# A fourth group of seven products in the second pair of column blocks of two down projections

## The chip, the cores and the metric

The kernel runs on one core of one Trainium2 chip. Times are device microseconds (us) of one execution; the time of a kernel is the median over runs. The engines are named as in the profile: PE (matrix engine), PEld (its weight loads), DVE (vector engine), ACT (scalar engine), POOL (GpSimd) and SP (issues most transfers). Each engine works through its own queue in order; semaphores connect them.

## The reference, cut to what matters

One layer on 256 rows of width 2048, all in float32: a half-weighted feed-forward network (FFN), a mixer, a second such network, and a gated embedding. The change touches the down projection `@ w_down` of both networks.

```python
def swiglu(h, w_gate, w_up, w_down):
    return (jax.nn.silu(h @ w_gate) * (h @ w_up)) @ w_down

x = x + 0.5 * swiglu(rms_norm(x, ffn1_norm[i]), ffn1_w_gate[i], ffn1_w_up[i], ffn1_w_down[i])
...
x = x + 0.5 * swiglu(rms_norm(x, ffn2_norm[i]), ffn2_w_gate[i], ffn2_w_up[i], ffn2_w_down[i])
```

The hidden width is 5632, the output width 2048. A down projection is thus 256 x 5632 times 5632 x 2048.

## The kernel before

**Three matmuls for one product.** Every float32 operand is split into a high part that PE takes (ACT copies it, line 182) and a low part, the rest (DVE subtracts, line 185). A product is then high x high, low x high and high x low: three matmuls, each 128 x 128 weights against 128 x 512 columns. The weights of the model are the moving operand; they are split on the fly, in tiles of 128 x 1024 (two k tiles of 512 columns), with names `whi`/`wlo` or, from a second ring, `shi`/`slo`. The rings hold four and three such pairs.

**Quarters and column blocks.** The 5632 hidden entries are 11 "quarters" of 512 (four k tiles of 128); the 2048 output columns are four blocks of 512, done in two pairs. One transfer of 1 MB brings one quarter of one block into a `raw` tile (lines 343 and 557). There are five `raw` buffers; during a down stage two of them hold the rows of x that the result is added to, so three are left for weights.

**Two ways to do a quarter.** As *columns* (`column`, line 660): for one block, each half of the quarter is split once and used by both row tiles, 12 matmuls a half, 24 a block, 48 for both blocks, with 4 splits. As a *group* (`chunk`, line 635): both blocks together, by a scheme of Strassen's kind, with 7 products instead of 8, each of 6 matmuls, 42 in all. For it DVE makes three sums of weight tiles (t1, t2, t4, line 550), POOL adds a fourth one by an accumulating transfer (line 643), and all seven right-hand sides are split. The left-hand sums of a quarter are made by `sum_forms` (line 487): four small DVE operations (line 496) and a split. The tiles for t1, t2, t4 and for these left-hand sums (`rows`) share two buffers. The products add into eight banks of PSUM, numbered 1 to 8; the columns of the first block use banks 2 and 4, those of the second 3 and 8, the same ones as the groups, so that both ways add up.

**The plan of a stage.** In `ffn`, `plans` lists the order for each of the two pairs of blocks: `("c", k)` does quarter k as columns, first block then second; `("s", k)` as a group; `("f", k)` makes the left-hand sums for k ahead of time. The last entry closes the stage: in the second pair it is `("a", (5, 6, 7, 8))`, the first block over quarters 5, 6, 7, 8 and then the second over 8, 7, 6, 5. After the last group `opened` (line 811) takes the banks 1, 5, 6 and 7 out: one ACT copy and eight DVE operations of 512 columns. `end` adds the remaining banks of a block to x and starts the next stage's preparation of it.

The hidden activations are split per quarter by `act` (line 803; a DVE row `hlo<-hT`), and `kept` holds the last two quarters. The sums of quarters 1 and 2 are kept from the first pair of blocks; that of quarter 0 is made again.

**What sets the order.** The code is traced in program order, with `step()` between pieces of work, at which work put off earlier (`put_off`) is traced. A scheduler then orders the instructions of each engine: by program order, except where an instruction would have to wait and a later one need not, and except for those pinned to program order. On SP the transfers of weights and those of the turned activations share one queue.

Of the kernel before, what the change touches and what calls it, by code (L numbers as in the profile page):

```python
# [33 lines left out]
def layer_kernel(ctx: ExitStack, tc: tile.TileContext, a: dict, shapes: dict, out: bass.AP):  # L34
# [47 lines left out]
    def small(n=8):  # L82
        return smp.tile([P, 8], F32, tag="sm", name=uid("sm"))[:, :n]
# [24 lines left out]
    def put_off(steps, fn, *args):  # L108


        def g():
            for _ in range(steps):
                yield
            fn(*args)

        return start(g())
# [370 lines left out]
    def sum_forms(pool, u, kind="n"):  # L487

        sums = pool.tile([P, 2, NB], F32, tag="sum", name=uid("rows"), bufs=2)
        s = sums.rearrange("p j n -> p (j n)").rearrange("p (z j x b) -> p z j x b", z=4, j=2, b=32)  # L490
        (a11, a21), (a12, a22) = ([u[:, k : k + 2, 4 * t : 4 * t + 4] for t in range(TT)] for k in (0, 2))
        for z, (x, y, op) in enumerate((
            (a21, a22, ALU.subtract), (s[:, 0], a11, ALU.subtract),
            (a11, a21, ALU.subtract), (a12, s[:, 1], ALU.add),
        )):
            nc.vector.tensor_tensor(out=s[:, z], in0=x, in1=y, op=op)
        both = halves(kind)
        split(*both, sums.rearrange("p j n -> p (j n)").rearrange("p (z t) -> p z t", z=4))
        return both
# [175 lines left out]
    def ffn(i, xn, nxt, bg=None):  # L675
# [7 lines left out]
        side = ExitStack()  # L683
# [18 lines left out]
        for f in range(NF):  # L702
# [9 lines left out]
            if f >= early or f in alone:  # L712
# [17 lines left out]
                s = Seven(xn, lambda kb: sums[kb], ((wg, f * NB), (wu, f * NB)), sevens, turns)  # L730
# [69 lines left out]
        def rows(k):  # L800
            return hT[k // 2][:, k % 2 * 4 : k % 2 * 4 + 4]
# [6 lines left out]
        def gather(x, ps, scale):  # L808
            nc.vector.scalar_tensor_tensor(out=x, in0=ps, scalar=scale, in1=x, op0=ALU.mult, op1=ALU.add)

        def opened(s, n):
# [5 lines left out]
            for t in range(TT):  # L817
# [9 lines left out]
                ("c", 10),  # L827
            ),
            (
                ("c", 10), ("c", 9), ("s", 2), ("c", 3), ("s", 1), ("f", 0), ("c", 4), ("s", 0), ("a", (5, 6, 7, 8)),  # L830
            ),
        )
        parts, forms = {}, {}
# [13 lines left out]
        for n in range(0, ND, 2):  # L847

            def end(side):
                m = n + side  # L850
                for t, z in enumerate(((2, 4), (3, 8))[side]):
                    gather(xt[t][m], s.bank(z), 0.5)
                put_off(0 if m == ND - 2 or m == ND - 1 and m < nxt.early else 2, nxt.block, m)

            s = Seven(kept, summed, ((wd, n * NB), (wd, (n + 1) * NB)), sevens, turns)
            plan = plans[n // 2]
            left = sum(kind == "s" for kind, _ in plan)
            for kind, kb in plan:
                final = (kind, kb) == plan[-1]
                if kind == "f":  # L860
                    forms[kb] = sum_forms(sevens, rows(kb))
                    continue
                if kind == "s":
                    left -= 1
                    s.chunk(kb, () if left else shared)
                    if not left:
                        put_off(0, opened, s, n)
                    continue
                for side in range(2):
                    s.column(side, (kb,) if kind == "c" else kb[:: 1 - 2 * side], final)  # L870
                    if final:
                        end(side)
        pools.close()
# [737 lines left out]

    n1, nm, n2, npl = Normed("ffn1_norm", load_turned), Normed("mix_norm"), Normed("ffn2_norm", kinds="hhnn", late=0), Normed("ple_norm", late=0)
    ffn(1, n1, nm, s5_prep)

    w_in = a["w_in"]
# [75 lines left out]
    mix.close()  # L1691

    ffn(2, n2, npl)


# [62 lines left out]
    with sums_phase("sums3") as sevens:  # L1758
        forms = {1: sum_forms(sevens, whole_rows(sevens, npl(1)), "h")}
        s = Seven(npl, forms.get, ((wg, 0), (wg, NB)), sevens, sevens)  # L1760
# [31 lines left out]
    s = small(1)  # L1792
# [157 lines left out]
```

## Time and profile before

| | us |
|---|---|
| median of three runs | 1808.87 |
| their range | 1808.36 to 1809.96 |
| the profiled execution, whole | 1808.1 |
| its span, first to last instruction | 1806.3 |

The profile is of one execution. Its span is the time from the first instruction to the last; 1.8 us of the execution lie around it. The second pair of the first down stage runs from 587.2 to 702.8 us of the span, that of the second one from 1584.8 to 1700.4.

To read its rows: a timeline row is start, duration, engine, line, operation, output<-inputs, shape and count, then in brackets the idle time just before it and what ended that. Durations of PE and DVE overlap with the next instruction's, so rates are read from starts. A windows row gives the busy time of each engine in a stretch, the number of its instructions, then the granted PE clock, the DMA share and GB/s.

### The profile page before, as it was taken

The page shows a single profiled execution, that of the slowest core. Times are in us where ns is not written, and L with a number is a line of the kernel's source. Part 1 is how long each engine was busy: PE and PEld are TensorE (multiplying, and loading weights), DVE is VectorE, ACT ScalarE, POOL GpSimd, SP SyncE. Part 2 cuts the span into 40 slices and gives each one's busy share as a digit, 9 for nine tenths or more (in the row PEclk, how much of TensorE's full clock was granted, in tenths as well). Part 3 has the DMA queues.
Part 4 walks back from the last instruction along what each step waited for, and adds up shares of the span by engine and source line. Part 5 has one row for each costly group of instructions (what it writes and reads, how often), then busy time and mean ns, then how long its engine had stood idle before and what let it go on. Part 6 is the DMA issues. An engine that isn't in the chain of part 4 may idle for free.

```text
span 1806.3 us, 24268 instructions
## 1 busy us (share of the span) xinstructions
PE 1799.4 (100%) x8890; PEld 1492.0 (83%) x8890; DVE 1615.7 (89%) x1894; ACT 1083.6 (60%) x1263; POOL 134.6 (7%) x196
## 2 busy tenths in 40 slices
PE   9999999999999999999999999999999999999998
PEld 7888888888888888888898888888888888888887
DVE  7998889999999898887867899999999999989875
ACT  7445455555566666466895566555565566666664
POOL 0020100000000001122121000000000000000000
PEclk9999999999999999999999999999999999999999
DMA  9689967687776667765646777776767786666663
GB/s 377 215 280 312 278 219 235 237 273 216 262 253 225 209 245 230 254 243 182 202 153 209 242 284 239 262 261 228 234 233 240 244 273 242 233 210 220 208 245 128
DMA packets 108518, 430.49 MB, mean 238 GB/s; under 512 B 24592, under 2 KB 48432, under 8 KB 66000
## 3 DMA queue, kind: packets, MB, share of 16 engines
q1 hardware_dynamic: 95952, 390.10, 61.1%
q0 software_dynamic: 12160, 38.55, 9.9%
q8 instruction: 69, 1.13, 0.3%
q14 instruction: 49, 0.40, 0.1%
q10 hardware_dynamic: 288, 0.31, 0.1%
HBM read 372.41 MB, written 10.88 MB: 212 GB/s over the span
## 4 chain that ended last, share of the span: by engine, by line
PE 99%; DMA 0%; DVE 0%; ACT 0%; SPq 0%; issue 0%; DVEq 0%; ACTq 0%
PE acc L358 31%; PE acc L353 16%; PE aux L358 15%; PE aux L353 8%; PE acc L539 5%; PE acc L544 5%; PE acc L542 5%; PE aux L544 4%; PE aux L539 4%; PE aux L542 4%; PE aux L1328 0%; PE acc L1585 0%; PE acc L1580 0%; PE acc L1576 0%; DMA raw<-in_head 0%; PE aux L1273 0%
## 5 line engine op out<-in xcount | busy, mean ns | idle before, releaser
L185 DVE TENSOR_TENSOR wlo<-raw,whi 128x1024 fp32r<-128x1024 f32 x478 | 576.4, 1221 | 94.0 <-ACT whi L182 90.7
L182 ACT CAST whi<-raw 128x1024 fp32r<-128x1024 f32 x478 | 495.8, 1050 | 271.2 <-PE acc L358 156.6
L358 PE MATMUL acc<-whi,nhi 128*128 128x512 f32 x852 | 332.7, 392 | 1.0 <-ACT whi L281 0.9
L358 PE MATMUL acc<-whi,nlo 128*128 128x512 f32 x852 | 330.4, 389 | 0.0
L353 PE MATMUL acc<-wlo,nhi 128*128 128x512 f32 x852 | 241.3, 390 | 0.0
L185 DVE TENSOR_TENSOR slo<-raw,shi 128x1024 fp32r<-128x1024 f32 x186 | 226.4, 1217 | 11.6 <-ACT shi L182 11.3
L182 ACT CAST shi<-raw 128x1024 fp32r<-128x1024 f32 x186 | 195.2, 1049 | 51.5 <-DMA raw<-in_ffn_w_down 24.0
L358 PEld LDWEIGHTS acc<-whi,nhi 128*128 128x128 f32 x852 | 159.8, 188 | 35.4 <-ACT whi L281 1.5
L353 PEld LDWEIGHTS acc<-wlo,nhi 128*128 128x128 f32 x852 | 159.7, 188 | 33.8 <-DVE wlo L185 0.4
L182 ACT CAST whi<-sum 128x1024 fp32r<-128x1024 f32 x83 | 87.5, 1054 | 166.2 <-DVE sum L550 154.4
L358 PEld LDWEIGHTS acc<-whi,nlo 128*128 128x128 f32 x852 | 159.9, 188 | 32.6 <-DVE nlo L282 0.2
L182 ACT CAST shi<-sum 128x1024 fp32r<-128x1024 f32 x61 | 64.3, 1053 | 103.8 <-DVE sum L550 99.8
L643 POOL DMA_DIRECT2D raw<-raw x47 | 41.4, 880 | 1032.5 <-DVE sum L550 782.0
L550 DVE TENSOR_TENSOR sum<-sum,raw 128x1024 f32<-128x1024 f32 x96 | 117.1, 1220 | 0.9
L185 DVE TENSOR_TENSOR wlo<-sum,whi 128x1024 fp32r<-128x1024 f32 x83 | 101.2, 1222 | 3.1 <-ACT whi L182 2.2
L358 PE MATMUL aux<-whi,nhi 128*128 128x512 f32 x244 | 95.0, 389 | 0.0
L358 PE MATMUL aux<-whi,nlo 128*128 128x512 f32 x244 | 94.9, 389 | 0.0
L185 DVE TENSOR_TENSOR slo<-sum,shi 128x1024 fp32r<-128x1024 f32 x61 | 74.5, 1221 | 0.7
L353 PE MATMUL aux<-wlo,nhi 128*128 128x512 f32 x244 | 75.1, 389 | 0.0
L550 DVE TENSOR_TENSOR sum<-raw,raw 128x1024 f32<-128x1024 f32 x48 | 58.5, 1220 | 3.6 <-DMA raw<-in_ffn_w_down 3.4
L539 PE MATMUL acc<-whi,hhi 128*128 128x512 f32 x154 | 60.2, 391 | 0.0
L542 PE MATMUL acc<-whi,hlo 128*128 128x512 f32 x154 | 60.0, 389 | 0.0
(420 smaller groups left out, 3531.9 us busy)
## 6 DMA issues: line engine op xcount, KB each, us to landing
raw<-in_ffn_w_down SPq DMA_DIRECT2D x88, 1024.0 KB, 4.9
raw<-in_ffn_w_gate SPq DMA_DIRECT2D x87, 1024.0 KB, 7.4
raw<-in_ffn_w_up SPq DMA_DIRECT2D x87, 1024.0 KB, 5.6
raw<-in_w_in SPq DMA_DIRECT2D x32, 1024.0 KB, 5.2
raw<-raw POOLq DMA_DIRECT2D x50, 512.0 KB, 5.6
raw<-in_w_out SPq DMA_DIRECT2D x16, 1024.0 KB, 5.0
raw<-in_w_ple_gate SPq DMA_DIRECT2D x16, 1024.0 KB, 5.0
hT<-mid SPq DMA_DIRECT2D x160, 64.0 KB, 4.7
```

Of the source, the lines that this page charges most:

```text
L182: copy = nc.scalar.copy(hi, src)
L185: rest = nc.vector.tensor_tensor(out=lo, in0=src, in1=hi.bitcast(F32), op=ALU.subtract)
L353: nc.tensor.matmul(ps[t], lhsT=lh, rhs=lo[:, j, cols], start=False, stop=stop and j == 1)
L358: nc.tensor.matmul(ps[t], lhsT=(ahi, alo)[i][:, 2 * h + j, t * P : (t + 1) * P], rhs=hi[:, j, cols], start=start and j == 0 and i == 0, st ...
L539: nc.tensor.matmul(ps, lhsT=lh[j], rhs=hi[:, j], start=begin and j == 0, stop=False, skip_group_check=joined)
L542: nc.tensor.matmul(ps, lhsT=ll[j], rhs=hi[:, j], start=False, stop=False, skip_group_check=joined)
L544: nc.tensor.matmul(ps, lhsT=lh[j], rhs=lo[:, j], start=False, stop=z in final and j == 1, skip_group_check=joined)
L550: nc.vector.tensor_tensor(out=t, in0=x, in1=y, op=ALU.add)
L643: nc.gpsimd.dma_start(b12, b22, accum_op=ALU.add)
```

## The change

Only the second plan and the loop that reads it change.

```diff
             (
-                ("c", 10), ("c", 9), ("s", 2), ("c", 3), ("s", 1), ("f", 0), ("c", 4), ("s", 0), ("a", (5, 6, 7, 8)),
+                ("c", 10), ("c", 9), ("s", 2), ("c", 3), ("s", 1), ("f", 0), ("o", 4), ("s", 0), ("o", 6), ("f", 5),
+                ("s", 5), ("a", ((7, 8), (8, 7, 6, 4))),
             ),
...
-                for side in range(2):
-                    s.column(side, (kb,) if kind == "c" else kb[:: 1 - 2 * side], final)
+                for side in range(1 if kind == "o" else 2):
+                    s.column(side, kb[side] if kind == "a" else (kb,), final)
                     if final:
                         end(side)
```

Quarter 5 is done as a group, with its left-hand sums made just before it. A new kind `("o", k)` does a quarter as columns for the first block alone; quarters 4 and 6 are done so, before group 0 and before group 5. The closing entry then has quarters 7 and 8 for the first block and 8, 7, 6, 4 for the second. Every quarter is still done once for each block. `opened` follows group 5, which is now the last group.

## The prediction

> **What bounds the kernel now.** First the page's head, its clock and its chain.
>
> ```profile
> span 1806.3 us, 24268 instructions
> PE 1799.4 (100%) x8890; PEld 1492.0 (83%) x8890; DVE 1615.7 (89%) x1894; ACT 1083.6 (60%) x1263; POOL 134.6 (7%) x196
> PEclk9999999999999999999999999999999999999999
> PE 99%; DMA 0%; DVE 0%; ACT 0%; SPq 0%; issue 0%; DVEq 0%; ACTq 0%
> ```
>
> The matrix engine is the whole chain, at full clock. A matmul less is time saved, but only while PE still finds its operands ready: every wait on PE is paid in full. So the next question is who feeds PE in the stretch that the change touches, the second pair of column blocks. It is 510 matmuls long in each down stage. I asked for windows: the first stage's stretch whole (from 587), and in each stage the piece around its last two groups of seven products.
>
> ```profile
> core 0: us, PE busy (x) PEld busy (x) DVE busy (x) ACT busy (x) POOL busy (x), PEclk, DMA share, GB/s
> 587.20:702.80 115.60, 115.60 (x511) 95.72 (x511) 100.59 (x106) 70.37 (x84) 4.64 (x5) 1.00 0.68 227
> 616.00:661.00 45.00, 45.00 (x200) 37.25 (x199) 44.53 (x47) 32.27 (x37) 1.78 (x2) 1.00 0.71 236
> 1617.00:1659.00 42.00, 42.00 (x187) 34.76 (x187) 41.84 (x42) 29.29 (x31) 1.73 (x2) 1.00 0.73 236
> ```
>
> Over its whole stretch the vector engine is idle for 15 us (115.60 less 100.59), which looks like room. From 616 to 661, though, it is busy 44.53 of 45 us, and in the second stage 41.84 of 42. There PE never waits only because operands were prepared ahead. The figure to follow is this **lead**: the start of the first matmul that reads a low part, less the end of the DVE subtraction that made it. It is smallest at the fourth product of group 0, the one on t4. The timeline has both ends, for the first stage (PE, then DVE) and then for the second:
>
> ```profile
> 654.79 0.61 PE L544 MATMUL acc<-slo,hhi 128*128 128x512 f32 x2
> 656.15 0.61 PE L544 MATMUL acc<-wlo,hhi 128*128 128x512 f32 x2
> ```
>
> ```profile
> 639.92 1.22 DVE L185 TENSOR_TENSOR slo<-raw,shi 128x1024 fp32r<-128x1024 f32 x1
> 641.05 1.22 DVE L185 TENSOR_TENSOR wlo<-raw,whi 128x1024 fp32r<-128x1024 f32 x1
> ...
> 643.32 1.22 DVE L185 TENSOR_TENSOR wlo<-raw,whi 128x1024 fp32r<-128x1024 f32 x1
> 644.86 1.23 DVE L550 TENSOR_TENSOR sum<-raw,raw 128x1024 f32<-128x1024 f32 x1 [0.31 <-DMA raw<-in_ffn_w_down]
> ...
> 652.02 1.22 DVE L185 TENSOR_TENSOR slo<-sum,shi 128x1024 fp32r<-128x1024 f32 x1
> ...
> 655.44 1.22 DVE L185 TENSOR_TENSOR hlo<-hT,hhi 128x1024 fp32r<-128x1024 f32 x1
> ```
>
> ```profile
> 1648.71 1.23 DVE L185 TENSOR_TENSOR wlo<-sum,whi 128x1024 fp32r<-128x1024 f32 x1
> 1652.40 0.62 PE L544 MATMUL acc<-wlo,hhi 128*128 128x512 f32 x2
> ```
>
> Lead in the first stage: 654.79 - (652.02 + 1.22) = 1.55 us. In the second: 1652.40 - (1648.71 + 1.23) = 2.46 us. That is all the slack there is. The same rows give the real rates, which are less than the recorded durations because instructions overlap: six matmuls from 654.79 to 656.15 are 1.36 us, so 0.2267 each; a subtraction or addition over 1024 columns starts 1.13 us after the one before (639.92, 641.05), two of them 2.27 (641.05 to 643.32).
>
> **The change part by part.** *Quarter 5 becomes a group.* 48 matmuls become 42: per stage 6 x 0.2267 = 1.36 us off the chain, 2.72 us in both. That is all it can win.
>
> *What DVE gets for it.* Quarter 5 as columns needs 4 subtractions (two halves, two blocks). As a group it needs 3 additions and 7 subtractions, and the new "f" entry four small operations and one subtraction:
>
> ```profile
> 634.37 0.42 DVE L496 TENSOR_TENSOR rows<-rows,hT 128x256 f32<-128x256 f32 x1
> 634.70 0.42 DVE L496 TENSOR_TENSOR rows<-hT 128x256 f32<-128x256 f32 x1
> 635.04 0.42 DVE L496 TENSOR_TENSOR rows<-hT,rows 128x256 f32<-128x256 f32 x1
> 635.37 1.22 DVE L185 TENSOR_TENSOR hlo<-hT,hhi 128x1024 fp32r<-128x1024 f32 x1
> ```
>
> These start 0.33 apart, so "f" is 4 x 0.33 + 1.13 = 2.46 us, and DVE's balance per stage is 6 x 1.13 + 2.46 = +9.2 us, while PE's time shrinks by 1.36. Over the whole stretch that fits (100.6 + 9.2 against 114.2). Where it falls decides: it is worked out in two steps.
>
> *Step 1, ("c", 4) becomes ("o", 4).* Ahead of group 0, PE loses the 24 matmuls of the second block, 5.44 us; DVE loses two subtractions, 2.27, and in the first stage the 0.31 us wait for a load (three transfer buffers are free, and one tile less is in line before it). The cover shrinks by the difference. Lead at group 0's t4: 1.55 - 5.44 + 2.58 = -1.31 us in the first stage, 2.46 - 5.44 + 2.27 = -0.71 in the second. Negative means that PE waits. What a wait costs beyond that is seen at the one place late in the trace where PE waited for a subtraction:
>
> ```profile
> 1720.61 1.23 DVE L185 TENSOR_TENSOR wlo<-raw,whi 128x1024 fp32r<-128x1024 f32 x1 [2.53 <-ACT whi L182]
> ```
>
> ```profile
> 1721.89 0.73 PE L353 MATMUL acc<-wlo,nhi 128*128 128x512 f32 x2
> ```
>
> PE starts 0.05 us after DVE ends (1721.84), and the pair takes 0.73 us instead of the 0.62 above: 0.16 together. So 1.47 and 0.87 us. Afterwards the lead is 0.16.
>
> *Step 2, from group 0's t4 to group 5's t4.* PE has ("o", 6) and one group between: 24 + 42 = 66 matmuls, 14.96 us. DVE has one group, from 643.32 to 655.44 less the 0.31 wait = 11.81; two subtractions for ("o", 6), 2.27; the low parts of the hidden quarters 6 and 5 (as at 655.44), 2.27; and "f", 2.46. That is 18.81. The deficit, 3.85, uses up that 0.16 first and is paid with the 0.16 of the last restart: **3.85 us of waiting**, part of it already at group 5's t1 product. Around group 0 PE takes the products in the program's order, and nothing that it could do instead has its operands: they come later from the same DVE queue.
>
> *The tail.* `opened` follows the last group, so its copy and eight half-width operations move behind group 5, ahead of the same kind of column units as before; the two quarters "a" gives to the first block and the four of the second cover it. Is there another wait?
>
> ```profile
> 654.30 1.22 DVE L185 TENSOR_TENSOR wlo<-raw,whi 128x1024 fp32r<-128x1024 f32 x1
> ...
> 662.38 1.22 DVE L185 TENSOR_TENSOR wlo<-raw,whi 128x1024 fp32r<-128x1024 f32 x1
> ```
>
> ```profile
> 658.87 0.61 PE L544 MATMUL aux<-wlo,nhi 128*128 128x512 f32 x2
> ...
> 665.67 0.61 PE L353 MATMUL acc<-wlo,hhi 128*128 128x512 f32 x2
> ```
>
> At the group's last product the lead was 658.87 - 655.52 = 3.35, now it is 0.16 + (3.35 - 1.55) = 1.96, so 1.39 less. The smallest lead of the columns after it was 665.67 - 663.60 = 2.07, now 0.68: no wait, with little to spare. After that eight units of the second block need 2.72 us of PE and 1.13 of DVE each, and the lead recovers.
>
> *At nothing:* the loads (8 for the four groups and 14 for the columns, 22 as before), the hidden quarters turned into parts (11 times, as before), banks and gathers. One accumulating DMA more on POOL is covered by DVE's own queue; its bound is the third rival. ACT, busy 32.27 of 45 us, takes 3 + 1 copies more.
>
> **Sum.** First stage 1.47 + 3.85 - 1.36 = +3.96; second 0.87 + 3.85 - 1.36 = +3.36; together **+7.3 us**. Against the profiled execution's own time, 1808.1 (span 1806.3 and 1.8 around it), that is 1815.4; against the median of the three runs, 1808.87, it is **1816.2**. No row shows two groups with only 24 matmuls between them. The bounds are no wait at all, -2.7, and, with one subtraction more ahead of the columns in each stage (1.13 - 0.68 + 0.16 = 0.6 each), +8.5.
>
> [...] In the kernel's first 10 us PE idles for 2.05 us in pieces, and the clock stays granted in full:
>
> ```profile
> 0.00:10.00 10.00, 7.95 (x34) 6.37 (x35) 3.90 (x8) 4.91 (x8) 0.83 (x7) 1.00 0.79 281
> ```
>
> [...]
>
> **Rivals.** (1) *The waits vanish* (not slower): DVE's order is not the program's, and work without weights might run earlier. It decides from 1.31 + 3.85 = 5.2 us of it ahead of 616 (4.6 in the second stage). For it: DVE idles 1.15 + 2.90 us shortly before,
>
> ```profile
> 604.39 1.22 DVE L185 TENSOR_TENSOR slo<-raw,shi 128x1024 fp32r<-128x1024 f32 x1 [1.15 <-ACT shi L182]
> ...
> 615.14 1.23 DVE L185 TENSOR_TENSOR wlo<-raw,whi 128x1024 fp32r<-128x1024 f32 x1 [2.90 <-ACT whi L182]
> ```
>
> that is 4.05, less than is needed; against it: "f" needs one of the two sum tiles, which the groups themselves use, and the hidden parts have two pairs. It gives 1808.87 - 2.72 = 1806.1. (2) *Half of it:* only "f" finds such a place; 2.46 less in each stage, +2.4, 1811.3. (3) *A load is late as well:* group 5's second weight tile waits for the buffer of group 0's b12, which waits for its accumulating DMA. Landing times of these DMAs, then of the weight loads:
>
> ```profile
> DMA to landing us min/median/max: 4.5/5.6/9.1
> DMA to landing us min/median/max: 4.6/4.9/9.2
> ```
>
> With medians the tile is there near 657.8 (b12 done at 655.52 - 2.58 = 652.9, plus 4.9) and needed near 660.7 (643.32 - 2.58 + 18.81 + 1.13). Both at their longest make it up to about 4 us late: +8 in two stages, 1824. (4) *The clock halves* between the waits: 66 matmuls at twice 0.2267 are 15.0 us more per stage, and the 3.85 of step 2 go; +22 on my sum, 1838.
>
> **How the numbers follow.** Chances: forecast 0.60, (1) 0.12, (2) 0.16, (3) 0.09, (4) 0.03. About 0.2% (3.6 us) is what a measurement of this kernel can tell from no change. Slower by more: the forecast, (3) and (4), less a little for a forecast that comes out half: 0.70. Within: (1), (2) and that little, 0.28. Faster by more than 3.6 us is beyond what 12 matmuls can give: 0.02, for shifts elsewhere. The range runs from just below (2), 1808, to 1821, half-way into (3); it leaves out (1), (4) and half of (3), 0.19.
>
> **What would show it.** In the changed profile: 8878 matmuls; PE waits for DVE low parts at lines 544 and 353, three per stage, at group 0's t4 and group 5's t1 and t4, 5.3 and 4.7 us in all; DVE without idle time from 616 to past group 5; the clock at 1.00. The forecast is wrong if group 5's t4 product starts without a wait, or if the waits name a load, or if DVE did the small "rows" operations before group 1.

## The result, and the profile after

| | before | after |
|---|---|---|
| median of six runs each, us | 1808.56 | 1822.4 |
| their range | 1807.42 to 1809.96 | 1820.08 to 1823.61 |
| the profiled execution, whole | 1808.1 | 1822.4 |
| its span | 1806.3 | 1820.6 |

The ratio is 1.0078, with a 95% interval from 1.0068 to 1.0088: slower by 13.8 us. The sign was forecast. The size was not: 1816.2 was the forecast and 1821 the upper end of the range.

The page of the changed kernel, its head, its engines and the chain that ended last:

```profile
span 1820.6 us, 24261 instructions
PE 1803.4 (99%) x8878; PEld 1489.3 (82%) x8878; DVE 1632.8 (90%) x1916; ACT 1090.1 (60%) x1271; POOL 134.0 (7%) x198
PE 83%; DVE 9%; DMA 2%; issue 2%; SPq 2%; ACT 1%; DVEq 0%; ACTq 0%; POOLq 0%
```

The twelve matmuls are gone (8878). But the chain, which was PE for 99%, leaves PE for a sixth of its length, and besides DVE there are DMA and SPq (the queue of the SP engine) in it. To see where the 14.3 us of span came from, take the matmuls by number: the start of the n-th matmul after, less the start of the same one before (behind each changed stage six numbers lower). The times in the left column are those of the kernel before.

| stretch | us lost in it | forecast |
|---|---|---|
| ahead of the first changed pair of blocks | -0.7 | 0 |
| inside the first (587 to 703) | +2.7 | +3.96 |
| behind it, up to 762 | +6.6 | 0 |
| from there to the second (1584) | 0.0 | 0 |
| inside the second (1584 to 1701) | +3.2 | +3.36 |
| behind it, up to the end | +2.5 | 0 |

Inside the stages the forecast is about right: 6 us of 7.3. The other 9 us were lost right *behind* them, where the change alters no instruction. PE's busy time in three windows there, before and then after:

```profile
700.00:722.00 22.00, 22.00 (x103) 18.31 (x102) 21.20 (x34) 15.46 (x23) 4.52 (x9) 1.00 0.82 255
722.00:762.00 40.00, 40.00 (x235) 32.68 (x234) 31.61 (x32) 16.84 (x19) 5.80 (x5) 1.00 0.77 252
762.00:790.00 28.00, 28.00 (x273) 23.11 (x272) 24.13 (x30) 16.43 (x19) 7.08 (x5) 1.00 0.67 241
```

```profile
700.00:722.00 22.00, 20.63 (x94) 16.52 (x92) 19.77 (x28) 13.62 (x22) 2.63 (x5) 1.00 1.02 333
722.00:762.00 40.00, 39.78 (x231) 32.51 (x232) 31.90 (x39) 18.80 (x22) 2.56 (x4) 1.00 0.62 187
762.00:790.00 28.00, 25.50 (x250) 20.48 (x249) 20.76 (x26) 17.19 (x19) 3.38 (x4) 0.94 0.78 305
```

Before, PE never pauses there. After, it stops around 720 and at 765, and the granted clock of the last window is 0.94. Now the timeline's PE rows that waited longest inside the first stage and behind it:

```profile
663.95 0.50 PE L539 MATMUL aux<-whi,nhi 128*128 128x512 f32 x1 [1.48 <-ACT whi L182]
...
765.35 0.69 PE L358 MATMUL acc<-whi,nhi 128*128 128x512 f32 x1 [2.50 <-ACT whi L182]
765.84 0.63 PE L358 MATMUL acc<-whi,nlo 128*128 128x512 f32 x1
766.27 0.63 PE L358 MATMUL acc<-whi,nhi 128*128 128x512 f32 x1
```

From 765.84 to 768.83, matmuls start 0.427 us apart instead of 0.227, at a granted clock of 0.50 (765.49 to 768.90).

What does the work behind the stage wait for? DVE's rows that had idled, at the end of the first changed stage, before and then after:

```profile
692.79 1.22 DVE L185 TENSOR_TENSOR wlo<-raw,whi 128x1024 fp32r<-128x1024 f32 x1 [3.08 <-ACT whi L182]
698.10 1.69 DVE L197 SCALAR_TENSOR_TENSOR nlo<-h,gains,nhi 128x256 fp32r<-128x256 f32 x4 [2.95 <-ACT nhi L195]
```

```profile
695.18 1.22 DVE L185 TENSOR_TENSOR hlo<-hT,hhi 128x1024 fp32r<-128x1024 f32 x1 [1.24 <-ACT hhi L182]
701.73 2.36 DVE L185 TENSOR_TENSOR wlo<-raw,whi 128x1024 fp32r<-128x1024 f32 x2 [5.33 <-ACT whi L182]
```

After, DVE has nothing to do for 5.33 us, and the low part made at 701.73 is one of the next stage's weights, which PE reads from 705.7 on. DVE waits for a copy of ACT, and that for a load:

```profile
700.65 2.00 ACT L182 CAST whi<-raw 128x1024 fp32r<-128x1024 f32 x2 [5.50 <-DMA raw<-in_w_in]
```

So the next view is the queue that issues the loads, SP's, before and then after:

```profile
676.30 0.33 SPq L343 DMA_DIRECT2D raw<-in_ffn_w_down  x1
679.04 3.50 SPq L343 DMA_DIRECT2D raw<-in_w_in  x2
684.62 11.48 SPq L233 DMA_DIRECT2D h<-mid  x16
```

```profile
681.26 2.60 SPq L343 DMA_DIRECT2D raw<-in_ffn_w_down  x2
686.05 9.13 SPq L233 DMA_DIRECT2D h<-mid  x12
695.28 0.52 SPq L343 DMA_DIRECT2D raw<-in_w_in  x1
695.85 2.50 SPq L233 DMA_DIRECT2D h<-mid  x4
698.45 0.53 SPq L343 DMA_DIRECT2D raw<-in_w_in  x1
```

`in_w_in` are the next stage's weights; `h<-mid` are sixteen small transfers that turn the stage's own result for the next stage, about 0.7 us each in the queue. Before, the two loads stand ahead of the sixteen, at 679. After, they stand behind twelve and behind all of them, at 695.28 and 698.45: 16 us later, where PE itself is only 2 us later. At the second changed stage it is the same: the two loads stand ahead of the sixteen at 1675.65 before and behind twelve and sixteen of them at 1702.73 and 1705.78 after, 27 us later for the first, where PE is 11.7 us later.

### The profile page after: what moved, and what is told of

It is laid out like the page before. It is cut to its first block, busy times and chain, and to the rows that moved or that the text cites. A ratio compares the mean times of both kernels' runs of the same rounds, so it can differ in the third digit from the quotient of the medians.

```text
span 1820.6 us, 24261 instructions
## 1 busy us (share of the span) xinstructions
PE 1803.4 (99%) x8878; PEld 1489.3 (82%) x8878; DVE 1632.8 (90%) x1916; ACT 1090.1 (60%) x1271; POOL 134.0 (7%) x198
## 3 DMA queue, kind: packets, MB, share of 16 engines
q8 instruction: 69, 1.13, 0.3%
## 4 chain that ended last, share of the span: by engine, by line
PE 83%; DVE 9%; DMA 2%; issue 2%; SPq 2%; ACT 1%; DVEq 0%; ACTq 0%; POOLq 0%
PE acc L358 27%; PE acc L353 13%; PE aux L358 12%; PE aux L353 6%; PE acc L544 4%; PE acc L539 4%; PE acc L542 4%; PE aux L544 3%; PE aux L539 3%; PE aux L542 3%; DVE wlo L185 3%; DVE slo L185 2%; SPq L233 2%; DVE sum L550 1%; DMA raw<-in_ffn_w_down 1%
## 5 line engine op out<-in xcount | busy, mean ns | idle before, releaser
L182 ACT CAST whi<-sum 128x1024 fp32r<-128x1024 f32 x87 | 91.6, 1053 | 171.0 <-DVE sum L550 159.4
L550 DVE TENSOR_TENSOR sum<-sum,raw 128x1024 f32<-128x1024 f32 x100 | 122.0, 1220 | 0.9
L185 DVE TENSOR_TENSOR wlo<-sum,whi 128x1024 fp32r<-128x1024 f32 x87 | 106.1, 1221 | 3.2 <-ACT whi L182 2.2
```

Source lines behind the costliest of these rows:

```text
L182: copy = nc.scalar.copy(hi, src)
L185: rest = nc.vector.tensor_tensor(out=lo, in0=src, in1=hi.bitcast(F32), op=ALU.subtract)
L550: nc.vector.tensor_tensor(out=t, in0=x, in1=y, op=ALU.add)
```

## The experiments

The theory after this (**queue theory**): the stage is slower inside by the waits that were counted, and what is lost behind it is these loads. They are issued late because a transfer buffer comes free late, and so they get behind the sixteen small transfers in the same queue, whose order the scheduler sets. The first rival (**buffer theory**): the buffers are late because DVE lags, and the queue adds nothing. The second (**one ledger**): everything, behind the stage too, is the DVE work that the change added, so that less of it gives all back.

All medians are in us; "before" is the kernel before on the same chip in the same series. The last five columns are shifts as in the table above, in the profiled execution, whose own time is given, since it can lie a few us off the median. They end with the last matmul; in e13 another 1.1 us of the span's growth lies behind that.

| run | median (runs) | before | ratio, 95% | profiled | ahead | in 1 | behind 1 | in 2 | behind 2 |
|---|---|---|---|---|---|---|---|---|---|
| the change | 1822.4 (6) | 1808.56 | 1.0078 [1.0068, 1.0088] | 1822.4 | -0.7 | +2.7 | +6.6 | +3.2 | +2.5 |
| e1 first stage only | 1817.28 (4) | 1808.25 | 1.0055 [1.0039, 1.0072] | 1817.2 | -0.2 | +3.1 | +6.0 | 0.0 | -0.2 |
| e2 even spacing | 1819.87 (4) | 1808.25 | 1.0065 [1.005, 1.008] | 1819.49 | 0.0 | +1.7 | +5.7 | +2.2 | +1.6 |
| e3 turned transfers on POOL | 1826.46 (4) | 1808.25 | 1.0101 [1.0086, 1.0116] | 1826.0 | -1.0 | +2.8 | +1.5, then +8.2 | +2.6 | +3.7 |
| e4 without quarter 5's sums | 1817.81 (4) | 1808.25 | 1.0055 [1.004, 1.007] | 1820.46 | -0.1 | +1.3 | +8.3 | -0.1 | +2.7 |
| e6 two loads on POOL | 1814.86 (4) | 1807.68 | 1.0041 [1.0026, 1.0056] | 1816.08 | +0.1 | +2.9 | +1.0 | +2.4 | +1.3 |
| e7 `ua` transfers later | 1817.82 (4) | 1807.68 | 1.0056 [1.0041, 1.0071] | 1818.09 | -0.5 | +3.2 | +2.0 | +2.6 | +2.6 |
| e9 before, loads held back | 1812.48 (8) | 1807.68 | 1.0026 [1.0016, 1.0037] | 1813.87 | +0.8 | 0.0 | +0.6 | 0.0 | +4.4 |
| e10 spacing, sums and loads on POOL | 1818.22 (4) | 1807.68 | 1.0059 [1.0042, 1.0076] | 1817.02 | -0.6 | +4.5 | +0.6 | +4.4 | -0.2 |
| e12 before, two loads on POOL | 1809.62 (10) | 1808.0 | 1.001 [1.0, 1.0019] | 1808.92 | -0.8 | 0.0 | 0.0 | 0.0 | +1.4 |
| e13 spacing, two loads on POOL | 1814.67 (4) | 1808.0 | 1.0038 [1.0023, 1.0053] | 1813.02 | -0.9 | +1.7 | +0.8 | +2.2 | -0.2 |
| e14 no sums, two loads on POOL | 1810.83 (10) | 1808.0 | 1.0016 [1.0006, 1.0025] | 1810.9 | -0.4 | +1.1 | +0.6 | +0.3 | +0.5 |

**e1: the change in the first stage alone.**

```diff
+            if i == 2 and n:
+                plan = (*plan[:6], ("c", 4), ("s", 0), ("a", ((5, 6, 7, 8), (8, 7, 6, 5))))
```

> The change in the first network's down stage only. The second stage cost +3.2 inside and +2.5 behind it, so about 1816.5 us if the two stages are independent, with the piece at reduced clock in the S5 part still there. If the loss behind the first stage needed the second one, or if the slow clock came by chance, less than 1814 us.

The losses in and behind the first stage are there again, the low clock too (0.83 granted from 762 to 772, as in the change), and the second stage lost nothing. The two stages are separate.

**e4: less DVE work inside.** Quarter 5's left-hand sums are left out (those of quarter 0 stand in for them), 2.46 us of DVE a stage.

```diff
-                    forms[kb] = sum_forms(sevens, rows(kb))
+                    if kb != 5:
+                        forms[kb] = sum_forms(sevens, rows(kb))
+                    if n and kb == 0:
+                        forms[5] = forms[0]
```

> The changed kernel, but group 5 reads the left-hand sums of quarter 0, and those of quarter 5 are left out: four small DVE operations and one subtraction less, 2.46 us per stage, and one ACT copy. If the waits inside the stage are DVE's shortage, as the ledger of leads has it, each stage's waits fall by about 2.4 us, from 4.0 to 1.6 and from 4.6 to 2.2. Theory Q: the loads behind the stage still come too late, so about 4.8 us less in all or a little more, 1817 us. Theory B: the backlog is smaller by as much again, 1812 us or less. If DVE were not what the group waits for, nothing changes.

Inside the stages, +2.7 and +3.2 became +1.3 and -0.1: 4.7 us for 4.92 us of DVE work. In sum that is the prediction's ledger, a microsecond of DVE for a microsecond of PE; by stage it is not, with 1.4 and 3.4 us for 2.46 each. Behind the stages nothing came back, +8.3 and +2.7, where the profiled execution is the slowest of the four, at a mean granted clock of 0.998 (0.999 in the change). The median says the same without it: the loss over the kernel before went from 13.8 to 9.6 us, 4.3 less, no more than came back inside. The one-ledger rival falls.

**e2: the same work, spread more evenly.**

```diff
-                ("c", 10), ("c", 9), ("s", 2), ("c", 3), ("s", 1), ("f", 0), ("o", 4), ("s", 0), ("o", 6), ("f", 5),
+                ("c", 10), ("s", 2), ("c", 9), ("s", 1), ("c", 3), ("f", 0), ("s", 0), ("o", 4), ("o", 6), ("f", 5),
```

> The same work as in the changed kernel, the order of it changed: columns 10, group 2, columns 9, group 1, columns 3, group 0, the first block of 4 and of 6, group 5, so that 48 matmuls stand between two groups everywhere. By the ledger, from one group to the next PE then has 90 matmuls, 20.4 us, and DVE 18.6 us (21.1 where the sums of a quarter are made too), so the waits inside the stage all but vanish: net -1.4 to 0 us per stage instead of +2.7 and +3.2. What is left behind the stages is the same for theory Q (the last group ends at the same place, the loads come as late): about 1816 us. For theory B the backlog is the same work too: 1816 us. If the spacing is not what matters, 1822 us.

Missed in part: inside it lost less than the change, +1.7 and +2.2, but did not get down to a gain. By the plan, the expectation had counted two splits of hidden quarters ahead of group 5 where there are three (4, 6 and 5). Behind, it lost nearly as much as the change.

**e3: the sixteen small transfers on POOL's queue.**

```diff
-                    nc.sync.dma_start(
+                    queue.dma_start(
...
-                turn_quarters(out, mid, 4 if soon else 6)
+                turn_quarters(out, mid, 4 if soon else 6, nc.gpsimd if soon else nc.sync)
```

> The changed kernel, with the 16 transfers per block that carry turned rows of the last two blocks issued on POOL's queue instead of SP's, so that the next stage's weight loads have none of them in front. Theory Q (the 9 us lost behind the two down stages come from those loads standing behind the transfers on SP): the loads are issued as their buffers come free, the waits inside the stages stay (+2.7 and +3.2 us net), those behind them go: about 1814 us. Theory B (DVE simply carries its 9 us of extra work per stage into the next stage and is late there whatever the queue does): the same waits behind the stages, about 1822 us.

A miss, and a blunt experiment. Behind the first stage the loss went down to 1.5, as the queue theory has it. But the same helper turns activations ahead of the second network as well, and there 8.2 us were lost; behind the second stage it lost more than the change. It decides nothing by itself.

**e6: only the two loads on POOL's queue.** The clean form of the question: the sixteen transfers stay where they are, and the two loads that had got behind them are issued by another engine.

```diff
-        nc.sync.dma_start(raw[:, :nk, :], quarter(w, k0 // 4, n0))
+        (by.pop() if by else nc.sync).dma_start(raw[:, :nk, :], quarter(w, k0 // 4, n0))
...
+        by[:] = [nc.gpsimd] * 2
```

> The changed kernel, with the first two weight loads of the stage that follows each down stage issued on POOL's queue, so that they are past the turned-row transfers of SP; these transfers themselves are left alone (in the first attempt they moved, and those of another stage with them). Theory Q: the DVE gap of 5.3 and 5.7 us behind the stages goes, and with it nearly all that is lost there; the waits inside the stages stay, +2.7 and +3.2: about 1814.5 us. Theory B (DVE's backlog): 1822 us.

1814.86: what the queue theory gave. POOL's rows in the timeline, and DVE's idle times at the same place:

```profile
689.67 0.57 POOL L344 DMA_DIRECT2D raw<-in_w_in  x1 [27.86 <-DMA h<-mid]
691.98 0.56 POOL L344 DMA_DIRECT2D raw<-in_w_in  x1 [1.75 <-DVE wlo L185]
```

```profile
696.59 1.23 DVE L185 TENSOR_TENSOR wlo<-raw,whi 128x1024 fp32r<-128x1024 f32 x1 [1.61 <-ACT whi L182]
698.87 1.22 DVE L185 TENSOR_TENSOR wlo<-raw,whi 128x1024 fp32r<-128x1024 f32 x1
```

POOL idles 1.75 us ahead of the second load, until a DVE subtraction ends: that frees its buffer. For the first load the bracket names the landing of a small transfer; the subtraction that last reads its buffer ends at 689.30, 0.4 us ahead of the issue, as for the second (691.58). So the buffers do come 10 us later than before (689.67 against 679.04). In the change the same two subtractions end at 688.26 and 690.53, so there the queue adds 7 to 8 us (695.28 and 698.45). The 10 us cost almost nothing, +1.0 us behind the first stage; the queue's share on top cost 5.6 more. The buffer theory is half true, and the cheap half: a late buffer made the loads late enough to fall behind the sixteen transfers. Both were needed.

**e7: the next batch of small transfers, two steps later.** Further on in the changed kernel, the first load of the pair at 744.80 had been parted from the second, which got behind eight more small transfers (`ua<-ub`) to 759.18; the wait at 765.35 follows that one. SP's queue after:

```profile
744.80 0.52 SPq L343 DMA_DIRECT2D raw<-in_w_in  x1
753.59 0.51 SPq L1226 DMA_DIRECT2D ua<-ub  x1
754.19 0.53 SPq L1239 DMA_DIRECT2D m<-scr_m  x1
754.77 4.31 SPq L1226 DMA_DIRECT2D ua<-ub  x7
759.18 10.14 SPq L343 DMA_DIRECT2D raw<-in_w_in  x4
```

```diff
-        put_off(1, u_part, pool, n, ub)
+        put_off(1 + 2 * n, u_part, pool, n, ub)
```

> The changed kernel, with the second batch of ua transfers traced two steps later, which puts one more weight load ahead of it on SP's queue, as it stands before the change. If that load's place is what costs the wait of 2.7 us near 765 and the slow clock after it, 4.4 us go: about 1818 us. If the wait there is DVE's or PE's lateness of 4 us handed on, it stays: 1822 us.

Of the 6.6 us behind the first stage 2.0 were left; with this order both loads go out together, at 745.10, and PE does not stop at 765. So about 2 of those 6.6 us come right behind the stage, from the two loads behind the sixteen transfers, and 4.5 from this later load, 1.7 of them from the half clock. That one follows from the first delay: in e6, where only the first pair was moved, the same load (the 11th of `in_w_in`) went out at 746.93, ahead of the eight, and only 0.5 us were lost from 722 to 762.

**e9: the cause alone, in the kernel before.** Nothing is changed but the place of the two loads in SP's queue, put behind the twelfth and the sixteenth small transfer, as in the changed kernel.

```diff
-        nc.sync.dma_start(raw[:, :nk, :], quarter(w, k0 // 4, n0))
+        with tc.issue_after(behind.pop(0)) if behind else ExitStack():
+            nc.sync.dma_start(raw[:, :nk, :], quarter(w, k0 // 4, n0))
...
+        behind[:] = marks[-2:]
```

> The kernel before, with nothing changed in the down stages; only the first two weight loads of the stage behind each are put on SP's queue where the changed kernel has them, after 12 and after all 16 of the turned-row transfers. Theory Q: this alone costs most of what the change lost right behind the stages (2.2 us at 720 and 2.5 us at 1725), so about 1812 us, with a DVE gap of some 5 us before the first split of the new weights. Theory B: without group 5's extra DVE work nothing is late, 1808.5 us.

1812.48: 4.8 us without any of the change's matmuls, sums or waits. SP's queue at the second stage, and DVE's idle time that follows:

```profile
1692.01 0.52 SPq L347 DMA_DIRECT2D raw<-in_w_ple_gate  x1
1692.58 2.81 SPq L234 DMA_DIRECT2D h<-mid  x4
1695.49 0.52 SPq L347 DMA_DIRECT2D raw<-in_w_ple_gate  x1
```

```profile
1698.51 2.36 DVE L186 TENSOR_TENSOR wlo<-raw,whi 128x1024 fp32r<-128x1024 f32 x2 [5.01 <-ACT whi L183]
```

The total fits, though the eight runs lie from 1810.27 to 1814.59 and the profiled one is among the upper four. Its parts do not follow the change's: behind the first stage only 0.6 us were lost, behind the second 4.4. DVE has its full lead in the kernel before, and behind the first stage that is nearly enough for a load 14 us late; there the later load keeps its place too (742.4), so the change's 6.6 us behind the first stage were not reproduced.

**e12: control, the kernel before with the two loads on POOL.** The edit is that of e6.

> The kernel before, with the first two loads of the work behind each stage issued by POOL instead of SP. There they stand ahead of the 16 transfers of the turned activations already. Queue theory: nothing to gain and nothing to lose, 1807.7 +- 1.5 us. Rival (POOL's queue is the better place for these loads whatever stands ahead of them, and that is what the run with them on POOL gained): faster by 2 us or more. If it is slower by x, x is the price of the other queue, and belongs to what that run still lost behind the stages (1.0 + 1.3 us).

1809.62, 1.0010 [1.0000, 1.0019]: no gain. POOL's queue is no better place as such; what helped in e6 was getting out from behind the sixteen transfers. If anything it costs about a microsecond behind the second stage (+1.4), which may be what e6 lost there (+1.3).

**e10 and e13: the spacing of e2 together with the loads of e6.** e10 also had POOL make the sums of quarters 0 and 5; e13 leaves them on DVE.

```diff
-                    forms[kb] = sum_forms(sevens, rows(kb))
+                    forms[kb] = sum_forms(sevens, rows(kb), eng=nc.gpsimd if n else None)
```

> A version meant to keep the 12 matmuls: even spacing of the groups, the two loads behind each stage on POOL, and the four small operations that make the left-hand sums of quarters 0 and 5 on POOL instead of DVE (1.33 us less DVE each). Even spacing alone left net +1.7 and +2.2 us inside the stages; 2.7 us less DVE work makes that about -1 to 0 each, and the queue's share behind them goes: 1807 to 1809 us. If POOL takes so long over these sums that the group waits for them, 1812 us or more.

> The changed kernel with the even spacing of the groups and with the two loads on POOL; the sums stay on DVE. If the losses inside a stage and behind it are separate: inside as in the run with the spacing alone (+1.7, +2.2 us), behind as in the run with the loads alone (+1.0, +1.3): 1807.7 + 6.2 = 1813.9. The same kernel with quarter 0's and 5's sums on POOL took 1818.2; if its miss came from POOL making the sums, this one is about 4 us faster than that and has no wait of over 1.5 us at group 2's and group 0's fourth products; if it came from the spacing together with the loads, this one takes 1818 too.

e10 was a miss by some 10 us. e13 came out near what was expected, in the total (1814.67 for 1813.9) and inside both stages (+1.7 and +2.2), and has no long wait at the fourth products of groups 2 and 0. The two differ only in who makes the sums, and by 3.9 us (10.5 and 6.7 over the kernel before of their own series). POOL's rows of e10, and DVE's in the same stretch:

```profile
620.12 2.46 POOL L497 TENSOR_TENSOR rows<-hT 128x256 f32<-128x256 f32 x2 [3.71 <-DVE sum L551]
622.55 0.91 POOL L497 TENSOR_TENSOR rows<-rows,hT 128x256 f32<-128x256 f32 x1
623.54 1.59 POOL L497 TENSOR_TENSOR rows<-hT,rows 128x256 f32<-128x256 f32 x1
```

```profile
621.02 1.84 DVE L197 SCALAR_TENSOR_TENSOR nlo<-h,gains,nhi 128x256 fp32r<-128x256 f32 x2
622.79 1.75 DVE L185 TENSOR_TENSOR wlo<-sum,whi 128x1024 fp32r<-128x1024 f32 x1
624.46 1.75 DVE L185 TENSOR_TENSOR wlo<-raw,whi 128x1024 fp32r<-128x1024 f32 x1
```

The four small sums take POOL 5.0 us (620.12 to 625.13) for DVE's 1.33, and while they run, DVE's subtractions start 1.67 us apart instead of 1.13: 0.54 lost on each. The two small operations at 621.02 take 1.77 us from start to start instead of 0.80 (0.40 each at 626.14). Two of each kind in those 5 us lose 2.06 us, more than the 1.33 that DVE was spared.

**e14: both together.** Without quarter 5's left-hand sums (as in e4) and with the loads on POOL (as in e6).

> The changed kernel without quarter 5's left-hand sums (it takes those of quarter 0: 2.46 us of DVE less per stage, left out) and with the two loads on POOL. If the losses inside a stage and behind it are separate: inside as in the run without the sums (+1.3, -0.1 us), behind as in the run with the loads on POOL (+1.0, +1.3): 1807.7 + 3.5 = 1811.2. If what the sums cost comes back behind the stage whatever the queue (that run lost 8.3 and 2.7 there): 1815 or more.

1810.83 for 1811.2, with +1.1 and +0.3 inside the stages where +1.3 and -0.1 were expected. The two causes add: DVE work inside the stage, the place of the loads behind it. No version that computes everything beat the kernel before; the best are e6 and e13, 7 us behind it.

## Why the prediction was right and wrong

**The bound and the gain** held: 8878 matmuls, and the six that each stage has less are in its +2.7 and +3.2.

**Steps 1 and 2, the waits inside a stage**, held in sum, and less well in place. Forecast were 5.3 and 4.7 us of waiting; the gaps between PE's starts above 0.227 add up to 4.0 and 4.6. In the first stage group 0's t4 cost 0.5 instead of 1.47, in the second 1.3 instead of 0.87; the rest lies in group 5 and just behind, in the second stage at t1 and t4 as named (1.4 and 1.7), in the first mostly at t2 (1.8). Taking 4.92 us of DVE work out gave back 4.7 us (e4), and about 3.9 with the loads on POOL (e6 to e14), so the ledger held in sum. Why the first stage came out 1.3 us lower was not tried. The waits also have another name than forecast. The forecast named low parts of DVE; but for 0.2 us at group 0 of the first stage, PE's long waits in the groups, with that at 663.95 above, are for high parts:

```profile
650.04 0.74 PE L544 MATMUL acc<-slo,hhi 128*128 128x512 f32 x2 [0.20 <-DVE slo L185]
1656.15 0.50 PE L539 MATMUL acc<-whi,hhi 128*128 128x512 f32 x1 [0.99 <-ACT whi L182]
1669.04 0.50 PE L539 MATMUL acc<-whi,nhi 128*128 128x512 f32 x1 [0.78 <-ACT whi L182]
1674.78 0.50 PE L539 MATMUL acc<-whi,hhi 128*128 128x512 f32 x1 [1.47 <-ACT whi L182]
```

The cause is still DVE's queue: ACT can only copy t2 or t4 once DVE has added it, and the product's first matmul reads that copy. In the first stage t2's addition ends at 662.82, the copy follows, and PE goes on at 663.95:

```profile
661.60 1.22 DVE L550 TENSOR_TENSOR sum<-sum,raw 128x1024 f32<-128x1024 f32 x1
```

**The tail** ("no wait, with little to spare") was nearly right: 0.7 us in the first stage, at 677.82 and 680.16, nothing that counts in the second.

**Rivals (1) and (2)** fell as argued: the small `rows` operations ran behind group 0 (654.45 on), not in the idle time ahead of it. **Rival (3)** named a late load in the wrong place, group 5's, where no wait of PE names a transfer. **Rival (4)**, the clock, came true once in the change and small: one stretch at a granted clock of 0.50, at 765, with eight matmuls 0.427 us apart where the rival had 66 at twice 0.2267; some 1.7 us, not inside the stage.

**The step that failed is "At nothing: the loads"**, together with the end of the tail, "and the lead recovers". I counted the loads (22 as before) and not when they can be issued. A transfer buffer comes free with the subtraction that reads it (in e6 it ended 0.4 us ahead of the issue of each load). With fewer columns behind the last group, DVE has not caught up when the stage ends, so buffers come free late: 10 us, by e6. Behind the last group DVE first idles at 676.65 before and at 695.18 after. That the fewer columns do it is argued from the plan; no run changed them alone. Less DVE work in the groups does not mend that: without quarter 5's sums (e14) the first load goes out at 687.46, 8.42 us after that of the kernel before with PE 0.76 us late, and in e6 10.63 us after it with PE 2.97 us late: 7.7 us beyond PE's own lateness in both. I had asked of DVE's lead only whether PE would wait *within* the stage. What the lead also sets is when the next stage's loads start, and there they met sixteen transfers in the same queue. That was visible in the profile of before: the two loads at 679.04, filling SP until 682.5, and the first of the sixteen at 684.62 leave about 2 us of slack, against a lead that I myself had cut by 1.4 us and a PE that I had put 4 us late. The term was 0 in the sum; it measured 6.6 and 2.5 us, of which another place for the two loads gave back 5.6 and 1.2 (e6).

With that term at e6's and e13's values (about 1 us a stage) the forecast would have stood: e6's 1814.86 is 1.3 us from 1816.2. That it is so near is in part luck: e6 lost 5.3 us inside the stages where 7.3 was forecast, and 2.3 behind them where nothing was.

## What to carry to other kernels

When a change takes slack from an engine that feeds the bottleneck, follow the slack past the end of the stage: list what that engine's progress releases, transfer buffers above all, and look in the issuing queue at what stands right behind those transfers. A load that slips behind a batch of small transfers waits for what is ahead of it, so a small delay can be paid as a large one, and one such slip can push a later load behind the next batch: here the queue added 7 to 8 us to loads whose buffers came 10 us late, and the later load behind eight more transfers cost 4.5 of the 6.6 us. And price an idle engine's help by what it does to its neighbours before giving it work: in e10 2.06 us of DVE were lost for 1.33 spared.

## What was not expected of the hardware

**Half the clock after short pauses.** The change's pause of 1.48 us at 664 was followed by full clock, the same pause in e7 by half; one of 2.50 us at 765 was followed by half clock in the change, one of 2.66 us at 765 in e2 by full clock. Ten microseconds around each of the four, two for the change, then e7 and e2:

```profile
661.00:671.00 10.00, 8.39 (x35) 5.88 (x34) 10.00 (x10) 8.65 (x10) 0.00 (x0) 1.00 0.53 143
762.00:772.00 10.00, 7.50 (x26) 5.72 (x25) 9.91 (x11) 5.23 (x6) 3.38 (x4) 0.83 0.84 336
```

```profile
661.00:671.00 10.00, 8.48 (x29) 6.17 (x29) 10.00 (x9) 8.05 (x9) 0.15 (x1) 0.83 0.51 127
```

```profile
762.00:772.00 10.00, 7.07 (x30) 5.22 (x29) 9.91 (x11) 6.11 (x6) 3.38 (x4) 1.00 0.83 333
```

The stretches at half clock themselves, in the change and in e7:

```profile
765.49:768.90 3.41, 3.41 (x9) 2.63 (x10) 3.41 (x5) 2.75 (x3) 0.25 (x3) 0.50 0.85 360
```

```profile
665.02:668.43 3.41, 3.41 (x10) 2.62 (x9) 3.41 (x4) 3.13 (x5) 0.00 (x0) 0.50 0.02 5
```

Neither the length of the pause nor PE's idle time in the ten microseconds tells the cases apart: 1.61 us idle (the change, 661 on) and 2.93 (e2) at full clock, 1.52 (e7) and 2.50 (the change, 762 on) with half clock. What does was not shown. The cost was small: eight slow matmuls in the change, 1.7 us.

**DVE while POOL adds.** While POOL added tiles in e10, DVE's subtractions over 1024 columns took 1.67 us from start to start instead of 1.13 (rows of e10).

**A queue is paid in issue time.** Sixteen small transfers kept SP's queue for 11.5 us (684.62 on), about twice the 5.2 us that an `in_w_in` load of 1 MB takes from issue to landing by the page of the kernel before. One of them alone is short, with about 0.6 us to issue and 1.9 us to land (medians of the sixteen). But sixteen of them in a row ahead of a load add up, and moving two loads a stage to POOL took the loss over the kernel before from 13.8 to 7.2 us (e6).
